# A hybrid encoder block: the second gate and up product in quarters from row blocks 4 and 5 on, its token sums rounded sooner

## The chip, the core and the metric

The kernel runs on one core of a Trainium2 chip. A core has five engines that run side by side, each through its own list of instructions in the order in which the program issues them: TensorE (PE in the profile, PEld for its weight loads), VectorE (DVE), ScalarE (ACT), GpSimd (POOL) and SyncE (SP, which here only starts DMAs). They hand work to each other by semaphores. The metric is the time of one execution on the device in microseconds, the median of several. Lower is better.

## The reference

One encoder layer on 1024 tokens of 1024 features, all in float32:

```python
h = rms_norm(x, norm1_g); z = h @ w_in
a, gate, q, k, v = split(z)
x = x + concat([conformer_conv(a, gate, ...), neighbourhood_attention(q, k, v, rpb)]) @ w_out
h = rms_norm(x, norm2_g)
x = x + (silu(h @ w_gate) * (h @ w_up)) @ w_down
```

Only the last two lines matter here, and of them only the two products of `h` with `w_gate` and `w_up` (1024 x 2816 each).

## The kernel before

**Rounding.** Each operand of a large matmul is kept as a rounded part and a rest, both in the type that TensorE takes. `split` makes them: ScalarE casts (line 116, the profile's `CAST`), and VectorE or GpSimd subtracts the cast from the source (line 120). `mac` then issues three matmuls (lines 124 to 126): part times part, part times rest, rest times part.

**Seven products instead of eight.** `w_gate` and `w_up` are cut into 22 row blocks of 128 columns. For row block i the kernel forms [gate | up] of both token halves (512 tokens each) from a 2 x 2 scheme over the two halves of the 1024 features, with the seven products of Strassen's method in Winograd's form: m1 to m7. Each product is four `mac`s, that is 12 matmuls that stream 512 columns. The left sides are token blocks or sums of them (`sop`, in tiles that the profile calls h and S); the right sides are weight blocks or sums of them (`tsum`, formed by `t_sums`), rounded by `prep` into the tiles `t{i}{p}`. m6, m5 and m3 of a row block accumulate in one PSUM bank ("B"), m7 and m4 in another ("D"); between them VectorE reads the bank (`evac`).

**A second level.** m1 is a plain product of a token block with a weight block. From row block 4 on it is done for two row blocks together, once more in Winograd's form: seven parts, P1 to P7, each of two `mac`s that stream 256 columns (`part`). `FIRST_I` says from which row block on: 4 for m1, 6 for m2. Where m2 is not in parts it stands in the list of products, one for each row block, and ends in the bank "A" (the profile's `A<-h,t4m`).

The parts need, for each pair of row blocks and each of m1 and m2: a load of the four weight quarters (`qr{i}{m}`, on SyncE's queue), P1's rounding (`qa`), four sums (`qs`, line 1191, always VectorE), the rounding of the sums (`qb` for P6, `qc` for P7) and of a quarter (`qd` for P4). `prep_part` issues them; `QUAD_DVE` names the few whose subtraction VectorE does, GpSimd does the rest. They also need four token sums for each of m1 and m2, formed once by `tok_sum` (line 1220) and rounded once by `tok_split` into `tok4` (tiles `qT1`, `qT2`, `qT3`, and a quarter of h2 for the fourth). The subtraction of the second and fourth is VectorE's for m2, of the first and third GpSimd's.

**The order.** One loop runs over the list of products, numbered n. For each it issues the product, its evacuation (`evac`), what was left over (`late`, `extra`), then the parts that are due (`parts_at`), then the preparations (`prep`, with all tasks up to number n + 4), and last the token roundings that `TOK` names for that n. `PARTS` puts the parts of a pair around its first m6: for m1 seven, five and three products ahead of it, for m2 one ahead of it (P1, P6), right behind it (P2, P5, P7) and two later (P3, P4). Each engine keeps this order.

Product 27 is m3 of row block 3, and product 28 is m6 of row block 4. With `FIRST_I` at 6 the products of row block 4 are m6, m7, m2, m5, m4, m3 (28 to 33) and of row block 5 the same (34 to 39).

**Buffers.** All weight tiles named above but `qd`, and the token sums, share the tag "G" with 21 buffers; a new tile waits until an older one has been read for the last time.

The names that the prediction's steps use: the evacuations of m3 (line 1408), m4 (lines 1380, 1381 and 1384), m5 and m7 (line 1404), m6 (line 1395), the product with the activated gate (line 1409), the evacuation of a part (line 1262 on ScalarE, 1264 on VectorE), `t_sums` (line 1143), and the sums that are stored (line 1432).

Of the kernel before, what the change touches and what calls it, by code (L numbers as in the profile page):

```python
# [65 lines left out]
def body(tc, a):  # L66
    from contextlib import ExitStack
    with ExitStack() as ctx:
        build(ctx, tc, a)


def build(ctx, tc, a):
# [1060 lines left out]
    def t_sums(i, ns):  # L1133
        (b11, b21), (b12, b22) = lr(raw_gu[i, 0]), lr(raw_gu[i, 1])
        for n in ns:
            if n in (1, 3):
# [12 lines left out]
    products += [(i, p) for p in ("m7", "m4", "m6", "m5", "m3") for i in range(2)]  # L1149
    PARTS = {"m1": {-7: ("P1", "P6"), -5: ("P2", "P5", "P7"), -3: ("P3", "P4")},  # L1150
             "m2": {-1: ("P1", "P6"), 0: ("P2", "P5", "P7"), 2: ("P3", "P4")}}
    FIRST_I = {"m1": 4, "m2": 6}
    parted = lambda i, p: i >= FIRST_I.get(p, FB)
    products += [(i, p) for i in range(2, FB) for p in ORDER if not parted(i, p) and (i > 3 or p not in ("m1", "m2"))]

# [66 lines left out]
    def tok_split(m, n):  # L1222
# [3 lines left out]
        else:  # L1226
# [2 lines left out]
        split(*tok4[m, n], tok_raw[m, g][:, c], (dve if (m, n) in TOK_DVE else pool,))  # L1229

    TOK = {17: [(tok_split, "m1", 2)], 18: [(tok_split, "m1", 1)], 19: [(tok_split, "m1", 3)], 21: [(tok_split, "m1", 4)],
           31: [(tok_split, "m2", 3)], 33: [(tok_split, "m2", 1)], 34: [(tok_split, "m2", 2)], 37: [(tok_split, "m2", 4)]}

    def part(m, i, p):
        j = (m, i)
# [416 lines left out]
```

## Time and profile before

| what | value |
|---|---|
| median of 3 runs | 1011.15 us (1010.62 to 1011.25) |
| the profiled execution's own time | 1010.8 us |
| its span, first to last instruction | 1009.0 us |
| granted TensorE clock, mean | 1.000 |
| busy: TensorE, VectorE, ScalarE, GpSimd | 1004.0, 782.0, 475.9, 458.6 us |

The stage of the gate and up products begins at 382.10 us of the span with m1 of row block 0; the pair of row blocks 4 and 5 runs from 464.38 us on. In the timeline each row is a start, a duration, the engine, the line, the operation, the tile written and those read, and the engine's idle time before it with what ended it. Tile names lose their last digits there, so `t4m` is any of row block 4's rounded weights, and `q60m` is a bank of the parts of the pair 6 and 7, of m1 or m2.

### The profile page before, as it was taken

Reading aid. Unit: us, or ns where it says so; the run is one execution under the profiler, and the core shown is the slowest. Engines: PE = TensorE matmul, PEld = TensorE weight load, DVE = VectorE, ACT = ScalarE, POOL = GpSimd, SP = SyncE. Lnnn points to the kernel's source line nnn. Section 1 sums busy time; section 2 is a strip of 40 time slices with the busy share of each in tenths; the row PEclk is TensorE's granted clock in tenths of the full one; section 3 lists DMA queues with packets and bytes.
Section 4 is the critical chain, followed back from the end, with each engine's and each line's share of the span. In section 5 each row is a group of like instructions: output and inputs, shape, how many; then the busy total and the mean of one; then the engine's idle time right before and its main releaser. Section 6 shows DMA issues by size and latency. Waiting matters only on the chain.

```text
span 1009.0 us, 15447 instructions
## 1 busy us (share of the span) xinstructions
PE 1004.0 (100%) x5442; PEld 841.3 (83%) x5442; DVE 782.0 (78%) x1232; ACT 475.9 (47%) x1038; POOL 458.6 (45%) x389
## 2 busy tenths in 40 slices
PE   9999999999999999999999999999999999999998
PEld 8888888887788888888888888888888888888887
DVE  5788997896979476987878778778678766768874
ACT  7556357837977245432443333433433452443432
POOL 1036675536873374374665566666665100003300
PEclk9999999999999999999999999999999999999999
DMA  9416783245515420234333443433441896634631
GB/s 351 174 42 216 214 228 108 87 161 182 167 49 195 182 84 21 84 105 146 135 137 126 142 131 124 156 132 109 157 136 50 279 363 221 205 105 131 223 115 42
DMA packets 75757, 151.71 MB, mean 150 GB/s; under 512 B 14473, under 2 KB 23561, under 8 KB 75041
## 3 DMA queue, kind: packets, MB, share of 16 engines
q1 hardware_dynamic: 73664, 147.20, 43.8%
q10 hardware_dynamic: 2016, 3.54, 0.9%
q8 instruction: 43, 0.70, 0.3%
q14 instruction: 34, 0.27, 0.1%
HBM read 112.07 MB, written 44.11 MB: 155 GB/s over the span
## 4 chain that ended last, share of the span: by engine, by line
PE 97%; POOL 1%; DMA 0%; issue 0%; ACT 0%; DVE 0%; POOLq 0%; ACTq 0%; DVEq 0%
PE B L124 6%; PE B L125 6%; PE B L126 6%; PE z L124 4%; PE z L126 4%; PE z L125 4%; PE D L124 4%; PE D L125 4%; PE D L126 4%; PE pj L124 3%; PE gl L124 3%; PE gl L126 3%; PE gl L125 3%; PE pj L126 3%; PE pj L125 3%; PE s L744 1%
## 5 line engine op out<-in xcount | busy, mean ns | idle before, releaser
L390 DVE SCALAR_TENSOR_TENSOR cv<-u,par,cv 128x1009 f32<-128x1009 f32 (+14 forms) x92 | 117.5, 1277 | 2.3
L1595 POOL TENSOR_TENSOR ou<-ou,resm 128x512 f32<-128x512 f32 x8 | 11.1, 1384 | 141.0 <-DVE ou L1586 126.5
L417 POOL TENSOR_TENSOR pa<-pa,pr 128x1022 f32<-128x1022 f32 (+5 forms) x24 | 58.0, 2418 | 37.4 <-ACT pr L416 37.0
L116 ACT CAST op<-sr 128x512 fp32r<-128x512 f32 x77 | 47.7, 619 | 57.2 <-PE B3d L126 26.4
L120 DVE TENSOR_TENSOR op<-sr,op 128x512 fp32r<-128x512 f32 x77 | 56.1, 728 | 17.8 <-ACT op L116 17.8
L116 ACT CAST op<-wd 128x512 fp32r<-128x512 f32 x54 | 33.5, 620 | 30.3 <-DVE wd L1490 19.5
L120 DVE TENSOR_TENSOR op<-wd,op 128x512 fp32r<-128x512 f32 x54 | 40.2, 744 | 2.1 <-ACT op L116 0.8
L1143 DVE TENSOR_TENSOR ts<-gu,ts 128x512 f32<-128x512 f32 x36 | 40.5, 1126 | 0.6
L771 ACT ACTIVATE e<-e,mx 128x341 f32<-128x341 f32 (+5 forms) x64 | 35.2, 553 | 8.9 <-DVE mx L766 8.9
L786 POOL TENSOR_SCALAR e<-e,rs 128x341 f32<-128x341 f32 (+5 forms) x64 | 32.8, 531 | 12.5 <-DVE rs L784 6.2
L1404 DVE TENSOR_TENSOR g<-D,g 128x512 f32<-128x512 f32 x22 | 15.2, 690 | 24.0 <-PE D L126 24.0
L444 ACT ACTIVATE sq<-z,r 128x64 f32<-128x64 f32 x96 | 28.2, 327 | 5.2 <-PE z L126 5.2
L766 DVE CUSTOM_DVE_ANT_0 e<-s,tab 128x341 f32<-128x341 f32 (+5 forms) x64 | 28.2, 476 | 2.8 <-PE s L744 2.7
L1381 ACT ACTIVATE D<-D 128x512 f32<-128x512 f32 x22 | 12.8, 582 | 35.8 <-DVE D L1380 35.8
L416 ACT ACTIVATE pr<-u,par 128x1022 f32<-128x1022 f32 (+5 forms) x24 | 27.0, 1138 | 1.7 <-ACT vs L474 1.7
L1097 POOL TENSOR_TENSOR sq<-sq,sq 128x512 f32<-128x512 f32 x12 | 17.6, 1465 | 16.5 <-ACT sq L1093 16.2
L744 PE MATMUL s<-kT,qT 64*128 64x341 f32 (+5 forms) x128 | 24.0, 454 | 0.0
L818 PEld LDWEIGHTS o<-e,vw 128*64 128x64 f32 (+1 forms) x336 | 18.1, 137 | 5.4 <-issue 5.1
L1093 ACT ACTIVATE sq<-xT 128x512 f32<-128x512 f32 x16 | 10.0, 632 | 25.3 <-DVE xT L976 25.2
L976 DVE TENSOR_TENSOR xT<-pj,xT 128x512 f32<-128x512 f32 x16 | 10.7, 682 | 14.3 <-PE pj L126 14.3
L444 ACT ACTIVATION_READ_ACCUMULATOR sq<-z,r 128x1 f32 x96 | 21.5, 224 | 0.0
L818 PE MATMUL o<-e,vw 128*64 128x128 f32 (+1 forms) x336 | 21.4, 277 | 0.0
(1508 smaller groups left out, 3785.4 us busy)
## 6 DMA issues: line engine op xcount, KB each, us to landing
gu<-in_gu SPq DMA_DIRECT2D x44, 512.0 KB
sr<-sd SPq DMA_DIRECT2D x77, 256.0 KB
sd<-sd SPq DMA_DIRECT2D x22, 512.0 KB
wd<-in_wd SPq DMA_DIRECT2D x36, 256.0 KB
sd<-g SPq DMA_DIRECT2D x33, 256.0 KB
x<-in_x SPq DMA_DIRECT2D x8, 512.0 KB
xT<-in_xp SPq DMA_DIRECT2D x8, 512.0 KB
xd<-xT SPq DMA_DIRECT2D x16, 256.0 KB
```

Of the source, the lines that this page charges most:

```text
L116: act.copy(hi, src)
L120: eng.tensor_tensor(*[w[..., sl] for w in (lo, src, hi.bitcast(F32))], OP.subtract)
L124: pe.matmul(acc, lh, rh, start=start, stop=False, skip_group_check=True)
L125: pe.matmul(acc, lh, rl, start=False, stop=False, skip_group_check=True)
L126: pe.matmul(acc, ll, rh, start=False, stop=stop, skip_group_check=True)
L390: dve.scalar_tensor_tensor(acc[:, o], uc[:, i], dwk[:, c, t:t + 1], acc[:, o], OP.mult, OP.add)
L417: pool.tensor_tensor(pa[:, o], pa[:, o], pr[:, o], OP.add)
L444: act.activation(sq[:, h * HD:(h + 1) * HD], z[:, h * HD:(h + 1) * HD], AF.Square, scale=r, accum_out=ss[:, h:h + 1])
L744: pe.matmul(s, qT[hh * HD:(hh + 1) * HD, hp, t * P:(t + 1) * P], k4[hh * HD:(hh + 1) * HD, hp, rh * 4:rh * 4 + AR[rh], c0:c0 + ncol], star ...
L771: act.activation(e, e, AF.Exp, bias=mx.pop((i, hh)), scale=-1.0, accum_out=sums[i][:, hh:hh + 1])
L818: pe.matmul(os_[s_][hh * HD:(hh + 1) * HD, hp], v[:n, c:c + HD], pTs[i][hh][:n, :, g], start=g == 0, stop=g == len(gs) - 1)
L1143: (pool if (i, n) in ON_POOL else dve).tensor_tensor(o, l, r, OP.subtract)
```

## The change

Two lines change. `FIRST_I` gets 4 for m2 as well, so that m2 of the row blocks 4 and 5 is no longer two products of 12 matmuls but seven parts of 6. Products 30 and 36 leave the list, and all later ones are numbered lower. `TOK` rounds the token sums of m2 behind the products 23, 24, 25 and 27 instead of 31, 33, 34 and 37, and in another order: second, first, third, fourth.

```diff
-    FIRST_I = {"m1": 4, "m2": 6}
+    FIRST_I = {"m1": 4, "m2": 4}
...
-           31: [(tok_split, "m2", 3)], 33: [(tok_split, "m2", 1)], 34: [(tok_split, "m2", 2)], 37: [(tok_split, "m2", 4)]}
+           23: [(tok_split, "m2", 2)], 24: [(tok_split, "m2", 1)], 25: [(tok_split, "m2", 3)], 27: [(tok_split, "m2", 4)]}
```

What follows from them without being written there: the pair's parts stand behind the products 27 (P1, P6), 28 (P2, P5, P7) and 30 (P3, P4). Their preparations are issued behind the products 21 (load), 25 (`qa`, the four sums, `qb`), 26 (`qc`) and 27 (`qd`). The two roundings of m2's weights for row blocks 4 and 5 go. The rounding of (4, m5) is issued behind product 26 instead of 27, and the load of the gate weights of row block 6 behind the sums for (4, m7) instead of the rounding of (4, m2).

## The prediction

> **What bounds the kernel now.** I read the page's busy shares and its chain first, then who made TensorE wait, then stretches of the stage, then the timeline of each engine around the pair of row blocks 4 and 5.
>
> ```profile
> PE 1004.0 (100%) x5442; PEld 841.3 (83%) x5442; DVE 782.0 (78%) x1232; ACT 475.9 (47%) x1038; POOL 458.6 (45%) x389
> ...
> PE 97%; POOL 1%; DMA 0%; issue 0%; ACT 0%; DVE 0%; POOLq 0%; ACTq 0%; DVEq 0%
> ```
>
> TensorE is busy all the time and carries 97% of the chain. In the view of waits (who waited for whom, us in total, times, longest) it has two entries:
>
> ```profile
> PE up L287 <- POOL ones L283: 1.1, 1, 1.1
> PE p L797 <- DVE mx L766: 0.4, 1, 0.4
> ```
>
> Both lie long before this stage. So matmul time that goes is saved in full, and whatever makes TensorE wait is lost in full: there is no slack to hide it. The table of stretches (length, then busy time of PE, PEld, DVE, ACT, POOL) shows how near the others are:
>
> ```profile
> 445.00:464.40 19.40, 19.40 (x102) 16.62 (x101) 14.33 (x21) 8.56 (x18) 15.82 (x12) 1.00 0.27 95
> 464.40:503.50 39.10, 39.10 (x199) 33.43 (x198) 34.10 (x48) 13.34 (x26) 20.74 (x15) 1.00 0.43 145
> 503.50:541.00 37.50, 37.50 (x207) 32.70 (x207) 28.53 (x50) 14.99 (x29) 20.95 (x16) 1.00 0.39 137
> ```
>
> In the first stretch, just ahead of the pair, GpSimd is busy 15.82 of 19.40 us and VectorE 14.33. That is where the change puts its preparations.
>
> **What the change removes: matmul time.** The starts of the first matmul of each group give the price of a product and of the parts:
>
> ```profile
> 464.38 0.39 PE L124 MATMUL B<-S,t4m 128*128 128x512 f32 x1
> ...
> 469.82 0.39 PE L124 MATMUL A<-h,t4m 128*128 128x512 f32 x1
> 472.54 0.39 PE L124 MATMUL B<-S,t4m 128*128 128x512 f32 x1
> ...
> 480.70 0.28 PE L124 MATMUL q60m<-h,qa6m 128*128 128x256 f32 x1
> 482.13 0.40 PE L124 MATMUL B<-S,t5m 128*128 128x512 f32 x1
> 484.88 0.39 PE L124 MATMUL D<-S,t5m 128*128 128x512 f32 x1
> 487.60 0.28 PE L124 MATMUL q60m<-h,qa6m 128*128 128x256 f32 x1
> 489.75 0.40 PE L124 MATMUL A<-h,t5m 128*128 128x512 f32 x1
> 495.22 0.28 PE L124 MATMUL q61m<-h,qc6m 128*128 128x256 f32 x1
> 496.65 0.40 PE L124 MATMUL D<-A,t5m 128*128 128x512 f32 x1
> ```
>
> One m2 takes 472.54 - 469.82 = 2.72 us; two take 5.44. The seven parts of a pair take 482.13 - 480.70 = 1.43 (P1, P6), 489.75 - 487.60 = 2.15 (P2, P5, P7) and 496.65 - 495.22 = 1.43 (P3, P4), 5.01 in all, and a product behind a run of parts takes 2.75 instead of 2.72 (484.88 - 482.13), three times 0.03. So 5.10 replace 5.44: **0.34 us saved**, not the eighth (0.68) that the count of columns promises, since 12 matmuls of 512 columns take 2.72 us and 12 of 256 take 1.43.
>
> The Trainium skill's page "TensorE: Matmul & The Clock Gate", section "Back-to-back issue gap", gives a warm gap of N/2.4 + 2.5 ns; by it the saving would be 24 x 215.8 - 42 x 109.2 ns = 0.59 us, an estimate of that page. The rows here (2.72/12 = 227 ns) decide.
>
> **What it adds ahead of the pair: GpSimd.** P1 now wants its weights at 464.38 and P6 0.71 later, at 465.1. GpSimd's list up to there:
>
> ```profile
> 455.20 1.28 POOL L120 TENSOR_TENSOR t3m<-ts,t3m 128x512 fp32r<-128x512 f32 x1
> 458.31 1.29 POOL L1143 TENSOR_TENSOR ts<-gu,ts 128x512 f32<-128x512 f32 x1 [1.83 <-DVE ts L1143]
> 460.33 1.29 POOL L120 TENSOR_TENSOR t4m<-ts,t4m 128x512 fp32r<-128x512 f32 x1 [0.73 <-ACT t4m L116]
> 461.58 1.74 POOL L1143 TENSOR_TENSOR ts<-gu,ts 128x512 f32<-128x512 f32 x1
> 464.00 1.30 POOL L120 TENSOR_TENSOR t4m<-gu,t4m 128x512 fp32r<-128x512 f32 x1 [0.68 <-ACT t4m L116]
> ```
>
> The subtraction for (4, m6) ends at 461.62. Behind it the change queues three: `qT1` (behind product 24), then `qa` and `qb` (behind 25), ahead of the sum that now starts at 461.58. What comes before is also later, because VectorE gets the subtraction of `qT2` (behind product 23) ahead of the sum on which GpSimd waits 1.83 us at 458.31: 0.61 us, with GpSimd idle beside it. So three subtractions start at about 462.2. Each takes 1.25 us from start to start when alone and 1.70 beside a busy VectorE (the 1.30 and 1.74 rows), and `qb` is done between 466.0 and 467.3: **P6 waits 0.9 to 2.2 us**; I take 1.4, between, as VectorE's sums are short. The removed subtraction (464.00) lies behind all this and helps nothing there.
>
> **VectorE.** The rows from the last time that this order ran:
>
> ```profile
> 450.55 1.14 DVE L1409 TENSOR_TENSOR g<-sl,g 128x512 f32<-128x512 f32 x1
> 452.21 1.18 DVE L1432 TENSOR_TENSOR sd<-g,sd 128x512 f32<-128x512 f32 x1
> 455.24 1.79 DVE L120 TENSOR_TENSOR t3m<-gu,t3m 128x512 fp32r<-128x512 f32 x1 [0.98 <-ACT t3m L116]
> 456.95 0.68 DVE L1404 TENSOR_TENSOR g<-D,g 128x512 f32<-128x512 f32 x1
> 459.11 0.42 DVE L1264 TENSOR_TENSOR g<-q42m,qu4m 128x256 f32<-128x256 f32 x1
> 459.45 0.70 DVE L1143 TENSOR_TENSOR ts<-gu 128x512 f32<-128x512 f32 x1
> 460.89 1.27 DVE L120 TENSOR_TENSOR t4m<-ts,t4m 128x512 fp32r<-128x512 f32 x1 [0.74 <-ACT t4m L116]
> 462.09 0.69 DVE L1380 TENSOR_TENSOR D<-D,u 128x512 f32<-128x512 f32 x1
> 464.58 0.69 DVE L1408 TENSOR_TENSOR g<-B,g 128x512 f32<-128x512 f32 x1 [1.80 <-PE B L126]
> 465.19 0.68 DVE L1384 TENSOR_TENSOR g<-D,g 128x512 f32<-128x512 f32 x1
> 465.78 1.31 DVE L1409 TENSOR_TENSOR g<-sl,g 128x512 f32<-128x512 f32 x1
> ```
>
> An operation of 128x512 takes 0.68 to 0.70, but 1.14 to 1.79 where both inputs are in SBUF (lines 120, 1143, 1409, 1432) and GpSimd is at work. The one at 455.24 ends at 457.03, 0.55 after GpSimd's of 455.20 ends at 456.48: it waited for it. Those with a PSUM input (456.95) stay at 0.68. The five slow rows above cost 0.44, 0.48, 1.09, 0.57 and 0.61 more, 0.64 in the mean. The Trainium skill says why, on the page "SBUF — State Buffer", section "Who interferes with whom": a VectorE instruction with two SBUF inputs contends with a GpSimd one that reads SBUF, and the later one waits for the whole of the other. It speaks against this change, and the trace agrees (the 0.55 above).
>
> P5 adds to the bank that P6 filled, so TensorE waits until VectorE has read P6 (line 1264). P5 would stand at 464.38 + 1.43 + 2.75 + 0.72 = 469.28. That read is queued behind all this on VectorE: four sums (0.34 each, as 459.11 to 459.45), the sum for (4, m7), its subtraction, m4's evacuation of row block 3, the subtraction for (4, m5), which the new numbers move from behind product 27 to behind 26, and the three evacuations of 464.58 to 465.78. ScalarE stands between them:
>
> ```profile
> 462.81 0.58 ACT L1381 ACTIVATE D<-D 128x512 f32<-128x512 f32 x1 [1.95 <-DVE D L1380]
> 463.31 0.61 ACT L116 CAST t4m<-gu 128x512 fp32r<-128x512 f32 x1
> 463.82 1.14 ACT L116 CAST t4m<-ts 128x512 fp32r<-128x512 f32 x2
> ```
>
> Step by step without any collision: 459.45 + 0.61 (`qT2`) = 460.06; sums to 461.42; the subtraction of (4, m7) 1.44 behind its sum, as in the rows, at 462.86; m4 at 463.47; the activation 0.72 later, then `qc`'s and (4, m5)'s casts 0.5 apart, the second done at 465.8; subtraction 465.9; three evacuations of 0.6; the read of P6 at 468.3, done at 468.7. That is in time by 0.5 us. But eight of these read SBUF twice (four sums, the sum, two subtractions, line 1409), and GpSimd's list (`qT1`, `qa`, `qb`, the sum of 461.58, `qT3`, `qc`, `qd`) leaves only the 0.73 of the row at 460.33 free. I let seven of eight collide: 7 x 0.64 = 4.5, the read done at 473.2, so **P5 waits until 473.25, 4.0 us behind its place**; P6's 1.4 is inside this. Bounds: none collides, 0; all eight by 1.09, 468.7 + 8.7 - 469.28 = 8.2.
>
> **Behind it.** VectorE should read P6 at 466.4 (behind 465.78) and does at 472.8: 6.4 late, 2.4 more than TensorE. It has 37.5 - 28.53 = 9.0 us free in a pair, 0.24 for each us, so 2.4 is gone in 10 us, four products; m5, m4 and m3 there each need a bank that it has read. Between 0 and 2.4; I take a third, **0.8**, as one product of 2.72 usually lies between.
>
> What moves at no cost: the load of the parts' weights (behind product 21 on SyncE's queue, four products before its use), ScalarE's added casts (8.56 busy of 19.40), the gate load of row block 6 (due six products later). The relief behind it (token roundings gone from products 31 to 37) is hidden, as TensorE does not wait there now.
>
> Sum: -0.34 + 4.0 + 0.8 = +4.5 us. The profiled run took 1010.8 us, span 1009.0; its sum is 1015.3. The median before is 0.35 higher: **1015.6 us**.
>
> **Rivals.**
> 1. Nothing waits, -0.34: 1010.8, not slower. For it: without collisions VectorE is 0.5 early, and `qT2`'s shift may be taken up elsewhere. Against: GpSimd needs three subtractions after 461.62, 465.4 at best, and P6 wants 465.1. It decides where GpSimd ends `qb` by 465.1 and VectorE reads P6 by 469.28.
> 2. Only GpSimd is late: VectorE collides less (two or three times), and P6's wait remains, 1.4: 1011.15 - 0.34 + 1.4 = 1012.2, from 1011.5 to 1013.2.
> 3. Buffers as well. Counting tiles of the tag "G" alive behind product 25, I get 23 for 21 buffers, 22 at the worst place before. A cast that waited so:
>
> ```profile
> 454.58 0.62 ACT L116 CAST t3m<-gu 128x512 fp32r<-128x512 f32 x1 [1.33 <-POOL h L120]
> ```
>
> Its source is a load, yet it waited for a GpSimd subtraction of another tile. Then `qc`'s cast waits until GpSimd has done `qT3` (466.5 + 2 x 1.25 to 1.70, 469 to 469.9) and (4, m5)'s for `qc` (1.9 to 2.3 more); the read of P6 is done near 475.7, 2.5 later than above: 1018.1, up to 1020.
>
> **How the numbers follow.** Forecast (1013.2 to 1017.5) 0.50, rival 1 0.13, rival 2 0.20, rival 3 0.17. About 0.2%, 2.0 us, is what a measurement of this kernel can tell from no change. No case saves 2 us: faster 0.01. Within: rival 1 and most of rival 2, 0.32. Slower: 0.67. The range leaves out rival 1 and the top of rival 3: 1011.2 to 1019.5.
>
> **What would show it.** Right: in the changed trace TensorE idles before the first P6 of `q41m` that reads `qb4m` of m2 (0.9 to 2.2 us, released by GpSimd line 120), and before P5 (released by VectorE line 1264); the stretch 445 to 464.4 shows GpSimd above 17 us; the parts of the pair still take 5.0 us without their waits. Wrong: no idle time at TensorE, or `qb` done by 465.1. It would also fail if VectorE's four sums take 0.42 each: then they met no GpSimd operation.

## The result, and the profile after

The changed kernel takes **1022.40 us** (median of 4 runs, 1022.14 to 1024.76) against 1011.19 for the kernel before: a ratio of 1.0121, 95% interval 1.0109 to 1.0134. It is 11.2 us slower; the forecast was 4.5 slower, and the time lies above its range. The profiled execution took 1022.31 us.

The page of the changed kernel: its head, busy times, granted clock and chain.

```profile
span 1020.5 us, 15518 instructions
...
PE 1007.2 (99%) x5460; PEld 843.3 (83%) x5460; DVE 782.7 (77%) x1241; ACT 477.4 (47%) x1042; POOL 461.8 (45%) x391
...
PEclk9999999999999999998999999999999999999999
...
PE 93%; POOL 3%; issue 2%; DVE 1%; ACT 1%; DMA 0%; POOLq 0%; ACTq 0%; DVEq 0%
```

No engine works noticeably longer: VectorE 782.7 us (782.0 before), GpSimd 461.8 (458.6). The span is 11.5 us longer and TensorE's share of the chain falls from 97% to 93%. So the time is waits, not work, and one slice of forty shows a lower clock. The view of waits names those of TensorE that are new in this stage (us in total, times, longest):

```profile
PE q41m L124 <- DVE qu4m L1264: 2.0, 1, 2.0
PE q40m L124 <- ACT qu4m L1262: 1.9, 1, 1.9
PE D L124 <- DVE g L1384: 1.8, 1, 1.8
PE q40m L126 <- POOL qa4m L120: 1.2, 1, 1.2
PE q41m L126 <- POOL qb4m L120: 0.7, 1, 0.7
PE B L124 <- DVE g L1404: 0.5, 1, 0.5
```

In order of time they stand ahead of P1's third matmul (1.2), P6's third (0.7), P2 (1.9), P5 (2.0), m3 of row block 4 (0.5) and m7 of row block 5 (1.8): 8.1 us in all. The table of stretches (length, busy time of PE, PEld, DVE, ACT, POOL with counts, granted clock, DMA share, GB/s) shows the rest:

```profile
472.74:478.80 6.06, 4.06 (x19) 3.77 (x19) 4.90 (x8) 2.83 (x6) 2.01 (x2) 0.53 0.23 87
478.80:482.09 3.29, 3.29 (x14) 2.68 (x14) 1.62 (x3) 0.00 (x0) 0.00 (x0) 0.82 0.31 77
...
488.99:493.98 4.99, 4.45 (x26) 3.75 (x24) 4.74 (x9) 1.41 (x4) 0.00 (x0) 1.00 0.28 108
493.98:501.09 7.11, 5.28 (x32) 4.37 (x30) 4.00 (x8) 4.15 (x9) 4.38 (x4) 1.00 0.42 149
...
464.04:513.57 49.53, 41.28 (x206) 34.66 (x205) 31.70 (x55) 15.15 (x29) 22.18 (x17) 0.93 0.29 101
```

Against the prices of the prediction (0.72 us for a part, 2.72 or 2.75 for a product) the pair's stage loses so much:

| from, to (us of the span) | without waits | after | lost |
|---|---|---|---|
| first P1 to first P5, 464.04 to 476.07 | 4.90 | 12.03 | 7.13 |
| P5, P7, m7 of row block 4, to 482.09 | 4.19 | 6.02 | 1.83 |
| parts of the next pair and m3, 488.99 to 493.98 | 4.18 | 4.99 | 0.81 |
| m6 of row block 5, three parts, to 501.09 | 4.87 | 7.11 | 2.24 |
| the m7 behind | 2.75 | 2.86 | 0.11 |

Together 12.1; less the 0.34 that the parts save, 11.8, which is what the stretch of 49.53 us is longer than the same work before (464.38 to 502.12, 37.74). The first row is the first four waits (5.9 us) and the slower matmuls around them. The second row is no wait: the matmuls of 256 columns start 0.21 us apart there instead of 0.12, and the clock reads 0.53 and 0.82 (0.50 over P5 and P7 alone). TensorE idled, and then ran at half speed.

**Why P2 and P5 stand still** is in the timelines of three engines (start, duration, engine, line, operation, tiles, idle time before it and what ended it). GpSimd, ScalarE and VectorE of the changed kernel:

```profile
465.56 1.72 POOL L120 TENSOR_TENSOR qb4m<-qs4m,qb4m 128x512 fp32r<-128x512 f32 x1
467.24 1.28 POOL L1143 TENSOR_TENSOR ts<-gu,ts 128x512 f32<-128x512 f32 x1
468.48 1.29 POOL L120 TENSOR_TENSOR qT3m<-qtm,qT3m 128x512 fp32r<-128x512 f32 x1
470.50 1.27 POOL L120 TENSOR_TENSOR qc4m<-qs4m,qc4m 128x512 fp32r<-128x512 f32 x1 [0.73 <-ACT qc4m L116]
```

```profile
469.80 0.62 ACT L116 CAST qc4m<-qs4m 128x512 fp32r<-128x512 f32 x1 [2.43 <-POOL qT3m L120]
471.80 0.62 ACT L116 CAST t4m<-ts 128x512 fp32r<-128x512 f32 x1 [1.38 <-POOL qc4m L120]
472.32 0.37 ACT L1262 COPY qu4m<-q40m 128x256 f32<-128x256 f32 x1
```

```profile
472.45 0.69 DVE L120 TENSOR_TENSOR t4m<-ts,t4m 128x512 fp32r<-128x512 f32 x1 [5.69 <-ACT t4m L116]
473.06 0.68 DVE L1408 TENSOR_TENSOR g<-B,g 128x512 f32<-128x512 f32 x1
473.66 0.68 DVE L1384 TENSOR_TENSOR g<-D,g 128x512 f32<-128x512 f32 x1
474.25 1.43 DVE L1409 TENSOR_TENSOR g<-sl,g 128x512 f32<-128x512 f32 x1
475.61 0.41 DVE L1264 TENSOR_TENSOR qu4m<-q41m,qu4m 128x256 f32<-128x256 f32 x1
```

The cast of `qc` reads `qs`, which VectorE finished long before, yet it waits until GpSimd has subtracted `qT3` from the token sums (469.77): another tile's last reader. The next cast, (4, m5), reads a sum and waits until GpSimd is done with `qc` (471.77). VectorE stands 5.69 us ahead of the subtraction that needs this cast. Behind it in its list are three evacuations and the read of P6, which ends at 476.02; P5 starts at 476.07. On ScalarE the copy of P1 stands behind the same cast, and that is P2's wait.

So two theories had to be told apart. **Buffers**: the casts wait for one of the 21 buffers. **Load**: GpSimd and VectorE are late by their own work and collisions, as the forecast had it, wherever the tiles lie.

### The profile page after: what moved, and what is told of

It is laid out like the page before. It is cut to its first block, busy times and chain, and to the rows that moved or that the text cites. A ratio compares the mean times of both kernels' runs of the same rounds, so it can differ in the third digit from the quotient of the medians.

```text
span 1020.5 us, 15518 instructions
## 1 busy us (share of the span) xinstructions
PE 1007.2 (99%) x5460; PEld 843.3 (83%) x5460; DVE 782.7 (77%) x1241; ACT 477.4 (47%) x1042; POOL 461.8 (45%) x391
## 4 chain that ended last, share of the span: by engine, by line
PE 93%; POOL 3%; issue 2%; DVE 1%; ACT 1%; DMA 0%; POOLq 0%; ACTq 0%; DVEq 0%
PE B L125 5%; PE B L124 5%; PE B L126 5%; PE z L124 4%; PE z L126 4%; PE z L125 4%; PE D L124 4%; PE D L125 4%; PE D L126 4%; PE pj L124 3%; PE gl L124 3%; PE gl L125 3%; PE gl L126 3%; PE pj L126 3%; PE pj L125 3%
```

## The experiments

Each time is the median of the runs; the kernel before, on the same chip and in the same session, took 1010.70 to 1010.91. Kernels are changed from the kernel after, unless it says otherwise. Where an edit inserts lines, all lines behind it count higher in that run's rows (line 1411 of no_rounding is line 1408).

### First: each suspect by itself

**sums_early** is the kernel before, with only the token sums rounded sooner.

```diff
-           31: [(tok_split, "m2", 3)], 33: [(tok_split, "m2", 1)], 34: [(tok_split, "m2", 2)], 37: [(tok_split, "m2", 4)]}
+           23: [(tok_split, "m2", 2)], 24: [(tok_split, "m2", 1)], 25: [(tok_split, "m2", 3)], 37: [(tok_split, "m2", 4)]}
```

> The kernel before with the token sums of m2 rounded early alone: the second, first and third behind the products 23, 24 and 25; the fourth stays behind 37, because it overwrites a quarter of h2 that the whole m2 still reads. m2 of row blocks 4 and 5 stays whole. If the early rounding is the harm (GpSimd late, buffers held), the time rises by several us. If it is harmless without the parts, within 1 us of the kernel before, about 1011 to 1012, and TensorE does not idle between 440 and 500 us.

1011.25 us, ratio 1.0007 (0.9997 to 1.0016), no new wait of TensorE in the stage. Rounding three of the four sums sooner costs nothing by itself.

**fewer_buffers** rounds the fourth sum behind product 23, which frees its source, and sends the load for row blocks 6 and 7 out two products later.

```diff
-            tasks += [(n - LEAD[q] - 0.5, (m, i, q)) for ...
+            tasks += [(n - LEAD[q] - 0.5 + 2 * ((m, i, q) == ("m1", 6, "load")), (m, i, q)) for ...
-           23: [(tok_split, "m2", 2)], ... 27: [(tok_split, "m2", 4)]}
+           23: [(tok_split, "m2", 2), (tok_split, "m2", 4)], ...}
```

> The changed kernel with two G buffers fewer alive behind product 25: the fourth token sum is rounded behind product 23 (it frees its raw tile there), and the load of the m1 quarters of row blocks 6 and 7 is issued behind product 27 instead of 25. Everything else, and all of GpSimd's and VectorE's work, is kept. Buffer theory: ScalarE's cast for qc no longer waits for GpSimd's qT3, nor the cast for (4, m5) for GpSimd's qc; VectorE's idle 5.69 us before the subtraction for (4, m5) falls below 2; P5 starts about 4 us sooner; 1014.5 to 1018. Collision theory (VectorE held up by GpSimd): nothing of that, 1021 to 1022.5. GpSimd's lateness at P1 and P6 (1.2 and 0.7 us) stays in both.

1020.59 us, ratio 1.0105 (1.0089 to 1.0122): a miss. ScalarE's timeline says why:

```profile
468.00 0.61 ACT L116 CAST qc4m<-qs4m 128x512 fp32r<-128x512 f32 x1
...
470.52 0.62 ACT L116 CAST t4m<-ts 128x512 fp32r<-128x512 f32 x1 [1.92 <-POOL qT3m L120]
```

The cast of `qc` no longer waits, but the next cast has taken over its wait, for the same `qT3`. P1 to P5 takes 10.43 us instead of 12.03.

**filled_waits** lets TensorE compute 10, 6, 16 and 18 matmuls of 256 columns into a spare bank ahead of P1, P6, P2 and P5, so that it does not idle.

```diff
+    FILL, filler = {"P1": 10, "P6": 6, "P2": 16, "P5": 18}, []
...
+            for _ in range(FILL[p]):
+                pe.matmul(filler[0][:, :256], sop["S1"][0][0][:, :P], sop["S1"][0][1][:, :256], start=True, stop=True)
```

> The changed kernel with TensorE kept busy in its four waits: 10, 6, 16 and 18 matmuls of 256 columns into a PSUM bank that nobody reads, ahead of P1, P6, P2 and P5 of the pair 4 and 5, 5.9 us of work for 5.9 us of waits. If the lower granted clock from 473 to 480 us comes from the idle time, the clock stays at 1.00 and the time falls by about 2 us, to 1020 to 1020.8. If the clock falls for another reason, no gain: 1022 to 1023.

1022.02 us, ratio 1.0113 (1.0098 to 1.0128). In the traced execution the clock stays at 1.00 through the whole stage, and P5 to the end of m7 takes 4.29 us instead of 6.02, as expected. The medians, though, differ by only 0.4 us, which is the band of no gain: two of the four executions, at a mean clock of 1.000, took 1021.1 and 1021.3 us, and two, at 0.998, took 1022.7 and 1023.5. So the filling did not always keep the clock, and its price (1.7 us) is shown by the trace and not by the times.

**parts_later** puts the pair's parts of m2 behind the products 28, 29 and 31, and the four roundings behind 22 to 24.

```diff
+    LATER = {0: ("P1", "P6"), 1: ("P2", "P5", "P7"), 3: ("P3", "P4")}
...
-            for o, g in at_.items() if parted(i, m) else ():
+            for o, g in (LATER if (m, i) == ("m2", 4) else at_).items() if parted(i, m) else ():
```

> The changed kernel with the seven parts of m2 of row blocks 4 and 5 one product later (behind the products 28, 29 and 31 instead of 27, 28 and 30; their preparations move with them) and the token sums of m2 rounded behind 22 (second, first), 23 (fourth) and 24 (third). Buffer theory: 22 buffers wanted at the worst place instead of 23, and none of them stands between P6 and its evacuation, so most of the waits go: 1012 to 1016. Collision theory: GpSimd and VectorE have the same work in the same stretch, so the waits stay within 2 us: 1020 to 1022.

1017.33 us, ratio 1.0064 (1.0049 to 1.0079), 1.3 above what was expected. The waits ahead of P1, P2 and P5 are gone. Others stand in their place:

```profile
PE D L124 <- DVE g L1385: 1.8, 1, 1.8
PE B L124 <- DVE g L1405: 1.3, 1, 1.3
PE B L124 <- DVE u L1396: 1.2, 1, 1.2
```

### Second: buffers alone

The next kernels keep every instruction, its engine, its order and its size. Only where one, two or three rounded token sums lie is changed: over the tile of the first product's, in place of a new buffer (later parts of m1 then read the wrong sums). **one_over** does it for T2, **two_over** for T1 and T2, **three_over** for T1 to T3; **four_fewer** adds the later load of fewer_buffers. The edit of two_over:

```diff
+        elif (m, n) in (("m2", 1), ("m2", 2)):
+            tok4[m, n] = tok4["m1", n]
         else:
             t = G(f"qT{n}{m}", F32R).rearrange("p (w k s) -> p w k s", w=2, s=256)
```

> The changed kernel with T2 of m2 alone written over T2 of m1: one buffer fewer is wanted (22 for 21 at the place of the stall, 21 for 21 at the later one). Buffers theory: one cast still waits for a buffer ((4,m5)'s, for GpSimd's last subtraction out of the token sums), so P5 still starts 3 to 5.5 us late, but the later wait ahead of D of (5,m7) is gone: 1017 to 1019.5. Load theory: as the changed kernel, 1021 to 1022.5.

> The changed kernel with one edit: the rounded token sums T1 and T2 of the second product (m2) are written over the first product's T1 and T2, which P5 and P6 of row blocks 4 and 5 have read by then, instead of into two new buffers of the common pool. Every instruction, its engine, its order and its size stay; only where two tiles lie changes, and two buffers fewer are wanted (21 for 21 where it was 23). (Later P5 and P6 of m1 read the wrong sums, so the output is not the reference's.) Buffers theory: qc's cast and (4,m5)'s cast no longer wait for GpSimd, VectorE's idle 5.69 us ahead of t4m goes, P2 and P5 start with no wait; P1's 1.2 and P6's 0.7 us (GpSimd) stay; the 1.8 us wait ahead of D of (5,m7) goes too, and with so little idling the clock keeps to 1.0: 1011.5 to 1014, near 1012.3. Collision or load theory (GpSimd and VectorE are late by their own work, wherever the tiles lie): the waits ahead of P2 and P5 stay near 3.9 us, 1019 to 1022.5.

> As the kernel with two tiles written over, and T3 of m2 over T3 of m1 too: three buffers fewer (20 wanted of 21). With one fewer (4,m5)'s cast came just behind qc's, which waited 2.41 us for GpSimd's last subtraction of the token sums (qT3); with two fewer qc's cast waits for nothing and (4,m5)'s cast takes over the wait for qT3 (1.90 us). Buffers theory, in its second form: a buffer that becomes free is handed to the next tile, so each buffer more moves the wait on by one tile; with the third (4,m5)'s cast gets a buffer whose readers are done, VectorE has its subtraction near 468.5, reads P6 by 470.5, and P5 waits for nothing: P1's and P6's 1.8 us stay, 1011.8 to 1015, near 1013. If the wait only moves on again (another late reader), or if VectorE's own work makes the read late: P5 waits 2 us or more, 1017.5 to 1020.

> The kernel with three tiles written over, and the load of the first product's raw weights of row blocks 6 and 7 sent out two products later: four buffers fewer at the stall. If three were enough: no difference beyond 1 us. If three were one short: 1011.8 to 1014.5 here against 1016 or more there.

| kernel | buffers fewer | median, us | ratio to before | first P1 to first P5, us |
|---|---|---|---|---|
| after | 0 | 1022.40 | 1.0121 (1.0109 to 1.0134) | 12.03 |
| one_over | 1 | 1019.88 | 1.0095 (1.0078 to 1.0112) | 10.98 |
| two_over | 2 | 1019.38 | 1.0085 (1.0067 to 1.0103) | 10.22 |
| three_over | 3 | 1016.60 | 1.0057 (1.0041 to 1.0074) | 8.45 |
| four_fewer | 4 | 1016.13 | 1.0052 (1.0037 to 1.0067) | 7.28 |

The last column is taken from the timeline of TensorE, the first matmul of P1 and that of P5; in after, then in four_fewer:

```profile
464.04 0.28 PE L124 MATMUL q40m<-h,qa4m 128*128 128x256 f32 x1
...
476.07 0.58 PE L124 MATMUL q41m<-qT1m,qb4m 128*128 128x256 f32 x1 [2.00 <-DVE qu4m L1264]
```

```profile
464.61 0.28 PE L124 MATMUL q40m<-h,qa4m 128*128 128x256 f32 x1
...
471.89 0.34 PE L124 MATMUL q41m<-qT1m,qb4m 128*128 128x256 f32 x1
```

Each buffer moves the stall on by a tile: in one_over `qc`'s cast still waits 2.41 us for `qT3`; in two_over `qc`'s does not and (4, m5)'s waits 1.90; in three_over neither does. From the timeline of ScalarE, in one_over, two_over and three_over:

```profile
469.88 0.62 ACT L116 CAST qc4m<-qs4m 128x512 fp32r<-128x512 f32 x1 [2.41 <-POOL qT3m L120]
```

```profile
467.21 0.61 ACT L116 CAST qc4m<-qs4m 128x512 fp32r<-128x512 f32 x1
469.73 0.62 ACT L116 CAST t4m<-ts 128x512 fp32r<-128x512 f32 x1 [1.90 <-POOL qT3m L120]
```

```profile
467.52 0.61 ACT L116 CAST qc4m<-qs4m 128x512 fp32r<-128x512 f32 x1
468.02 0.62 ACT L116 CAST t4m<-ts 128x512 fp32r<-128x512 f32 x1
```

My bands were missed for one, two and three buffers: I had counted that 21 wanted for 21 is enough. It was not: in two_over, at that count, (4, m5)'s cast got a buffer only when GpSimd had read it for `qT3`. The median of two_over even lies in the band of the load theory (1019 to 1022.5), though the wait ahead of P2 is gone, which that theory does not allow. Two of its executions, at a mean clock of 1.000, took 1017.7 us, and two, at 0.997, took 1021.0 and 1021.2, so the median stands between them. four_fewer is within 1 us of three_over, which was the sign that three are enough. In all, 6.3 us of median went with no instruction changed but the place of one load, which the load theory does not allow. But 5.4 us over the kernel before remain, which the buffer theory does not explain.

**before_g20** is the kernel before with 20 buffers instead of 21.

```diff
-        return T("G", [P, 1024], 21, name, dt)
+        return T("G", [P, 1024], 20, name, dt)
```

> The kernel before with 20 buffers in the common pool in place of 21, nothing else. By a count of the buffers wanted along its instructions it wants 22 at most (product 37) and 21 at products 19 to 21 and 41 to 45. If a lacking buffer by itself stalls TensorE in this kernel, also without the change: new waits of 1 to 3 us at those places, 1013 to 1020. If buffers only matter together with the change's fuller queues: 1010.5 to 1011.5.

1020.64 us, ratio 1.0097 (1.0082 to 1.0112): a lacking buffer costs 9.7 us with no change of the schedule. The pattern repeats ahead of P2 of m1 of this pair (at 454.12) and ahead of P2 of m2 of the next (at 514.87). The granted clock falls there too (0.88 over 450 to 464 us, 0.89 over 505 to 520), which is part of the 9.7. The two waits, and the casts around the first:

```profile
PE q60m L124 <- ACT qu6m L1262: 2.5, 1, 2.5
PE q40m L124 <- ACT qu4m L1262: 2.0, 1, 2.0
```

```profile
450.77 0.62 ACT L116 CAST t3m<-ts 128x512 fp32r<-128x512 f32 x1 [2.52 <-POOL qT3m L120]
...
455.98 0.62 ACT L116 CAST t3m<-ts 128x512 fp32r<-128x512 f32 x1 [1.40 <-POOL qc4m L120]
```

No run here has more than 21 buffers.

### Third: the queues

**two_over_p6** gives two_over's subtraction of `qb` to VectorE.

```diff
-    QUAD_DVE = {("m1", 6, "P1"), ...
+    QUAD_DVE = {("m2", 4, "P6"), ("m1", 6, "P1"), ...
```

> The kernel with two tiles written over, and the subtraction of P6's weights (qb of row blocks 4 and 5, 1.72 us on GpSimd) taken by VectorE. If the waits that are left ahead of P1 and P6 are GpSimd's queue: P6's 0.7 us goes, P1's 1.2 us stays (its subtraction stands before), 1010.9 to 1012, some 0.7 under the kernel with two tiles written over alone, unless VectorE's 0.7 to 1.7 us more make it late at the reads of P6 or P5. If these waits are not GpSimd's queue: no difference from it.

1020.37 us against 1019.38, not faster and far from the band. P6's wait goes, but P5's is 2.8 us and P2's 0.6: VectorE is the later one already.

**m5_on_pool** gives only the subtraction of (4, m5), ahead of which VectorE stood 5.69 us, to GpSimd.

```diff
-    ON_DVE = {..., (4, "m3"), (4, "m5"), (4, "m7"), ...}
+    ON_DVE = {..., (4, "m3"), (4, "m7"), ...}
```

> The changed kernel with the subtraction of (4,m5)'s weights on GpSimd in place of VectorE, nothing else: the buffers are as short as before and the cast waits as long, but VectorE does not stand behind it any more with three additions (2.8 us) and the read of P6 in its queue. Head-of-queue theory (what costs is that the waiting subtraction stands ahead of P6's read): P5's wait of 2.0 us goes, P2's 1.9 us stays (P1's copy is behind the same cast on ScalarE), the clock keeps nearer 1: 1018 to 1020. If the lateness of P6's read is VectorE's own load or collisions: as the changed kernel, 1021.5 to 1023.

1020.51 us, ratio 1.0096 (1.0081 to 1.0111), 0.5 above the band. P5's wait goes and P2's stays (2.4 us), as expected: P1's copy is still behind the waiting cast, and P6's read needs that copy.

**no_t1** is four_fewer with T1's rounding left out; **no_rounding** leaves out all four (its edit is shown; the load is two products later in both).

```diff
     def tok_split(m, n):
         g, c = TOK_AT[n]
+        if (m, n) in [("m2", n) for n in (1, 2, 3, 4)]:
+            tok4[m, n] = tok4["m1", n]
+            return
```

> The kernel with four buffers fewer, with the rounding of T1 of m2 left out (one cast, and 1.47 us of GpSimd just ahead of the subtractions of qa and qb; P5 takes m1's T1). GpSimd-queue theory: qa and qb are done 1.5 us sooner, P1's wait of 1.17 us goes to 0.0 to 0.1, P6's 0.70 to 0.2 to 0.5, the later waits of 0.4 and 1.0 stay: 1013.8 to 1015.2. If P1's wait is not GpSimd's queue: 1015.7 to 1016.7, as with T1.

> The changed kernel with the load two products later and none of the four token sums of m2 rounded (P4, P5, P6 and P7 of m2 take m1's): no early rounding is left on GpSimd, VectorE or ScalarE, and no buffers for it; what is left of the change is the quarters themselves for all pairs. Queue theory: P1 and P6 wait for 0 to 0.4 us together, P2 and P5 for nothing; the waits of 0.4 at (4,m3) and 1.0 at (5,m7), which come behind the quarters' own reads on VectorE, stay: 1012.5 to 1014.5. If early rounding isn't what makes P1 and P6 wait: over 1015.5. If the later waits are its doing too: 1010.4 to 1011.5.

no_t1: 1014.76 us, in its band, but not by its reason. P1's wait goes and P6's falls to 0.5, as said; yet P5 now waits 1.5, and from P1 to P5 it takes 7.25 us as against 7.28; its trace reaches P1 0.53 us sooner (464.08 against 464.61). no_rounding: 1016.39, outside its band. No wait for GpSimd is left, none for a buffer, and P5 still waits 2.4 us. VectorE's timeline in no_rounding:

```profile
459.72 1.55 DVE L1191 TENSOR_TENSOR qs4m<-qr4m 128x256 f32<-128x256 f32 x1
461.30 1.39 DVE L1191 TENSOR_TENSOR qs4m<-qs4m,qr4m 128x256 f32<-128x256 f32 x1
...
465.60 0.69 DVE L1383 TENSOR_TENSOR D<-D,u 128x512 f32<-128x512 f32 x1
467.98 1.36 DVE L120 TENSOR_TENSOR t4m<-ts,t4m 128x512 fp32r<-128x512 f32 x1 [1.69 <-ACT t4m L116]
...
470.46 1.25 DVE L1412 TENSOR_TENSOR g<-sl,g 128x512 f32<-128x512 f32 x1
471.63 0.41 DVE L1267 TENSOR_TENSOR qu4m<-q41m,qu4m 128x256 f32<-128x256 f32 x1
```

From 465.60 on it is the same list as in the changed kernel, with a wait of 1.69 us (the cast stands behind the activation of m4's bank on ScalarE) and no buffer in it. The read of P6 ends at 472.04, and P5's place is 464.64 + 4.90 = 469.54. So a second cause is the place of P6's read, behind that subtraction and the evacuations of product 27. By the rows, collisions are part of it, as five of these operations ran beside GpSimd and took longer than alone. Two of the four sums took 1.55 and 1.39 us (0.42 alone), the subtractions of (4, m7) and (4, m5) 1.02 and 1.36 (0.69 alone), line 1409's product 1.25 (0.68 alone): 3.7 us in a chain that leads to this read, more than the 2.56 by which P5 is late. No run takes the collisions away alone.

**no_rounding_no_add** also leaves out the two additions of g behind P3 and P4 of this pair.

```diff
+            if i > 4:
                 dve.tensor_tensor(sl[b], sl[b], gt[b][:, :512], OP.add)
```

> As the kernel without any rounding, and for row blocks 4 and 5 the two additions of g to sl behind P3 and P4 (0.70 us each on VectorE) left out. If the waits at (4,m3) and (5,m7) are VectorE's load with the quarters' reads: they fall together from 1.4 to under 0.5, 0.8 to 1.6 us below the kernel without rounding. If they come from something else (GpSimd's sums, buffers): within 0.4 us of it.

1016.85 us, no gain, but the wait it was made for is gone: ahead of m7 of row block 5 nothing stands any more (1.0 us in no_rounding), while 0.5 is left at m3 of row block 4. P2 and P5 wait 1.1 and 2.8 in this trace, more than in no_rounding. This run tells the place of the cause, not its price.

**no_rounding_m5**, **no_rounding_m5_no_add** and **four_fewer_m5** are no_rounding, no_rounding_no_add and four_fewer with (4, m5)'s subtraction on GpSimd, as in m5_on_pool.

> The kernel without any of the four roundings, with the subtraction of (4,m5)'s weights on GpSimd. Head-of-queue theory: VectorE goes from the addition for D (done near 466.3) straight to three additions (2.0 to 2.6 us) and reads P6 by 469.5, P5 waits 0 to 0.3 instead of 2.4 us: 1013 to 1014.2 (1016.4 with it on VectorE). If the read is late by VectorE's own work: 1015.5 or more.

> The kernel without rounding and with (4,m5) on GpSimd, and the two additions of row blocks 4 and 5 left out too. If buffers, the place of that subtraction in the queue and VectorE's load behind are the whole of the loss: the wait ahead of D of (5,m7) goes as it did before (1.0 to 0), about 0.5 us at (4,m3) is left, 1011.3 to 1012.6. If something else of the quarters costs: over 1013.

> The kernel with four buffers fewer and all the rounding, with (4,m5)'s subtraction on GpSimd. There P5 waited for nothing, since P1's and P6's waits for GpSimd (1.87 us) had put TensorE behind VectorE already. If these two causes lie side by side: no gain, 1015.4 to 1016.5, the GpSimd waits stay at 1.8 to 2.0. If they add up: 1014.5 or less.

no_rounding_m5: 1013.11 us, ratio 1.0021 (1.0011 to 1.0030); P1 to P5 takes 5.09 us. no_rounding_m5_no_add: **1011.61**, ratio 1.0008 (0.9999 to 1.0017). All that is left new of TensorE's waits in this stage:

```profile
PE B L124 <- DVE g L1408: 0.5, 1, 0.5
```

four_fewer_m5: 1015.29 against 1016.13, 0.1 below the band of no gain, the lowest run of each at 1015.2, and P1 to P5 takes 7.27 us as against 7.28. There VectorE reads P6 at 469.16 and GpSimd's 1.87 us ahead of P1 and P6 are what TensorE waits for. In no_t1 it is the other way round. GpSimd's lateness and VectorE's are worth 2.4 us (7.27 - 4.90) and 2.6 (no_rounding, 7.46 - 4.90) up to P5 and lie side by side: to take one of them away gains next to nothing there.

**mended** keeps the change and its computation, and adapts what stands around it: the parts as in parts_later, roundings behind 22, 24, 24 and 26, two loads later, six subtractions and sums on the other engine, the third pair's stores one product sooner.

```diff
-               (4, 2), (4, 4), (5, 1), (0, "m4"), (0, "m5"), (1, "m6")}
-    ON_DVE = {..., (4, "m3"), (4, "m5"), (4, "m7"), (5, "m5"), (5, "m6")}
+               (0, "m4"), (0, "m5"), (1, "m6")}
+    ON_DVE = {..., (4, "m3"), (4, "m6"), (4, "m7"), (5, "m5")}
...
+            SHIFT = {("m1", 6, "load"): 2, ("m2", 4, "load"): 1, ("m2", 4, "P1"): -1}
...
+           22: [(tok_split, "m2", 1)], 24: [(tok_split, "m2", 2), (tok_split, "m2", 4)], 26: [(tok_split, "m2", 3)]}
...
-        due = extra and p in ("m2", "m5", "m7", "m6", "m3")[:5 if parted(i, "m2") else 4]
+        due = extra and p in ("m2", "m5", "m7", "m6", "m3")[:5 if i > 2 else 4]
```

> The change kept, with its surroundings adapted (same computation): quarters of m2 of row blocks 4 and 5 behind products 28, 29 and 31, its token sums rounded behind 22, 24, 24 and 26, the two loads 1 and 2 products later, P1's weights one sooner, sums of row blocks 4 and 5 and (4,m6) on VectorE, (4,m5) and (5,m6) on GpSimd, the third pair's stores one product sooner. By the theory that all of the loss is queues and buffers and none of it the quarters themselves, it comes back to the kernel before: 1010.8 to 1014. If the quarters themselves cost (their short matmuls, their reads): not under 1016.

1014.76 us, ratio 1.0038 (1.0023 to 1.0053), 0.8 above the band: two thirds of the loss come back, no part waits any more, but its view of waits still has 2.9 us for VectorE's evacuations and reads. No version here beats the kernel before.

## Why the prediction was wrong, point by point

**What was right.** TensorE had no slack, and every wait was lost in full. The parts save 0.34 us: the stage without the losses of the table is that much shorter than before. With the 0.34 us by which the changed trace reaches the stage sooner, 12.1 - 0.34 - 0.34 = 11.4 of the 11.5 us of span are accounted for. GpSimd ended `qb` at 467.28 (the row of 465.56; said: 466.0 to 467.3), and TensorE waited 1.2 + 0.7 = 1.9 us for it (said: 0.9 to 2.2, though all ahead of P6 and not P1). That this wait lies inside P5's was said, and four_fewer_m5 and no_t1 show it. The read of P6 on VectorE ends the longest wait, as said. The direction was right.

**The step that failed** is "I let seven of eight collide: 7 x 0.64 = 4.5, the read done at 473.2, so P5 waits until 473.25, 4.0 us behind its place". P5 started at 476.07, 7.13 behind its place, and collisions were not what held it. VectorE's slow operations ahead of (4, m5)'s subtraction, in the changed kernel's timeline:

```profile
461.25 1.52 DVE L1191 TENSOR_TENSOR qs4m<-qr4m,qs4m 128x256 f32<-128x256 f32 x1
462.69 1.78 DVE L1143 TENSOR_TENSOR ts<-gu 128x512 f32<-128x512 f32 x1
...
465.28 0.86 DVE L120 TENSOR_TENSOR t4m<-ts,t4m 128x512 fp32r<-128x512 f32 x1 [0.81 <-ACT t4m L116]
```

They are 1.10, 1.09 and 0.17 us longer than alone (0.42 and 0.69), 2.4 in all, and then VectorE idled for 5.69: the loss was absorbed. Only the 1.43 of line 1409 lay on the path, 0.75 too long. So four of the eight took clearly longer than alone, not seven. (The row at 456.95, named for the operations with a PSUM input that stay at 0.68, shows nothing, as GpSimd was idle then; those of 462.09 and 464.58 do.) What held it was rival 3, to which I gave 0.17. Its mechanism is the trace word for word: `qc`'s cast waits for `qT3`, (4, m5)'s for `qc`, the read of P6 is done "near 475.7" (476.02 measured). The buffer ladder shows it: 12.03 us from P1 to P5 become 7.28 with four buffers fewer and the same instructions.

The rest of that step was not empty. In no_rounding, where no cast of this pair ahead of P5 waits for a buffer, P5 is still 2.4 us late, by VectorE's list with its collisions, as the forecast had it; I had this list ending at 468.7 without collisions, 0.5 early. The count of 23 tiles for 21 buffers was in my hands. I treated it as one case beside others, when a count over the limit says that some cast must wait. How long, and whether TensorE waits with it, the count leaves open: the kernel before wanted 22, and had no such wait of TensorE.

**Two sizes behind it.** "Behind it, 0.8" measured 0.81 + 2.24 + 0.11 = 3.2. Of the 2.24 some 0.8 is another buffer wait (1.8 us ahead of m7 of row block 5, 1.0 in each kernel of the ladder that wants fewer buffers), the rest VectorE with the two additions of each pair, since the wait goes with them. "One product of 2.72 usually lies between" did not hold: VectorE had the parts' four operations to do on top. And the clock, 1.83 us, was in no term.

**Rival 3's own time** (1018.1, up to 1020) was short by these: 7.13 instead of 6.5 up to P5, 3.2 instead of 0.8 behind, 1.8 of clock. That is 4.9 us; 1022.40 - 1018.1 is 4.3, as the changed trace reaches the stage 0.34 us sooner and its median stands 0.09 above its profiled time, not 0.35.

**The tests that I set.** TensorE idles ahead of the parts, released by GpSimd's line 120 and VectorE's line 1264: right. GpSimd above 17 us in the stretch ahead of the pair: wrong.

```profile
445.00:464.04 19.04, 19.04 (x100) 16.34 (x98) 16.30 (x23) 8.25 (x16) 15.08 (x12) 1.00 0.43 152
```

It was busy 15.08 of 19.04 us, less than before: of the three subtractions only `qT1`'s ran in the stretch (`qa`'s starts at 463.88, `qb`'s at 465.56), and the sum of 461.58 moved out of it, to 467.24, just ahead of `qT3`'s subtraction, for which `qc`'s cast waited. The parts without their waits: P3 and P4 took 1.43, as said; the others ran between waits or at the low clock. The sums: three of the four took 0.52, 0.43 and 0.42, one took 1.52.

**What stays open.** The wait at m3 of row block 4 was in every kernel with this change (0.3 us in mended, 1.3 in parts_later, about 0.5 in most) and was not taken apart. How much of VectorE's lateness is its place in the list and how much collisions was not separated. Nor was the 0.9 us between no_rounding_m5_no_add and the kernel before, whose interval reaches down to 0.9999.

## What to carry to other kernels

Work that is moved earlier lengthens the life of its tiles, so count the buffers at the busiest point before counting instructions; a count at the limit was already too many here, where the last buffer's last reader was late. A wait of a cast whose source is long done, ended by another engine's operation on a different tile, was a buffer wait here: look for the next operation in that engine's list and in that of its consumer, since all of them are late with it. And where two engines are late for the same instruction, test them together, for to mend one shows nothing.

## What the hardware showed

The granted clock falls to half after idling, and the same idle time does not always do it. In no_rounding a single wait of 2.40 us was enough, and in one_over 1.16 and 0.70 us within three were. In two_over 1.15, 0.71 and 2.61 us within ten were not, in the traced execution. Stretches from P2 on, first no_rounding, then two_over, and two matmuls of 512 columns of one_over behind its two waits, 0.43 us apart instead of 0.23:

```profile
468.82:474.83 6.01, 3.60 (x19) 3.40 (x18) 4.24 (x7) 1.11 (x3) 2.34 (x2) 0.75 0.61 221
```

```profile
470.67:475.80 5.13, 2.52 (x20) 2.31 (x19) 5.07 (x8) 2.62 (x6) 2.60 (x3) 1.00 0.38 147
```

```profile
468.75 0.63 PE L126 MATMUL B<-S,t4m 128*128 128x512 f32 x1
469.18 0.63 PE L124 MATMUL B<-S,t4m 128*128 128x512 f32 x1
```

In the changed kernel the fall cost 1.83 us from P5 on; the matmuls of P2, ahead of the wait of 2.00 us, already stood 0.21 us apart. In no_rounding the same stretch, P5 to the end of m7, took 1.45 us longer. The Trainium skill, page "TensorE: Matmul & The Clock Gate", section "What's actually happening", says that the clock is set by the activity in a free-running window of some 3.4 us, and is halved after an idle one. That the window runs freely would explain why the place of the wait decides, and one window at half speed would cost an estimated 1.7 us by that page. The traces agree with that price (1.83 and 1.45 us); but none of our waits was as long as a window, so a wholly idle window was not needed.
